# Six input weight columns: kept in DRAM for the second batch, or loaded and split again by it

## The chip, the core and the metric

The kernel runs on one core of one Trainium2 chip. The metric is the time of one execution on the device in microseconds. The engines are TensorE (PE; its weight loads are listed as PEld), VectorE (DVE), ScalarE (ACT), GpSimd (POOL) and SyncE (SP), which here only issues transfers. Each engine runs its own list of instructions in order and waits on semaphores for the others.

## What is computed

One layer of a hybrid encoder runs on two independent batches of 512 tokens, the prompt (b=0) and the sample (b=1), with the same weights. Cut to what matters here:

```python
mod = silu(c) @ w_ada + b_ada                     # (1, 6 * 1024)
sh1, sc1, g1, sh2, sc2, g2 = split(mod, 6)
h = rms_norm(x, norm1_g) * (1.0 + sc1) + sh1      # (512, 1024)
proj = h @ w_in                                   # w_in is (1024, 2816)
q_a, k_a, v_a, q_r, k_r, v_r, g_r = split(proj)   # 512, 128, 128, then 4 x 512 columns
o_a = windowed_attention(q_a, k_a, v_a, sink)
o_r = bidirectional_retention(q_r, k_r, v_r, g_r, decays)
x = x + g1 * (concat(o_a, o_r) @ w_out)
h = rms_norm(x, norm2_g) * (1.0 + sc2) + sh2
x = x + g2 * (square(relu(h @ w_mlp1)) @ w_mlp2)
y = rms_norm(x, final_g)
```

The first 768 columns of `w_in`, six blocks of 128, are the attention's: four of q, one of k, one of v. The change concerns these six blocks and nothing else.

## The kernel before, in words

**Products in three parts.** Every fp32 operand of a large product is split into two fp32r tensors, a high part (a cast of the value) and a low part (the value less the high part). A product is then three matmuls (`mm3`, lines 128 to 130): high by high, high by low, low by high. In the profile a weight block `k` therefore shows as `raw_k` (the load, line 89), `wh_k` (the cast on ScalarE, line 97) and `wl_k` (the subtraction on VectorE, line 103). The matmul at line 130 is the one that reads `wl`.

**The front.** For batch 0 the six attention blocks are computed first, in a front that goes through the 1024 rows of the weights in eight steps of 128 (`kc`). Each step loads one slab of 128 rows by 768 columns (`load_wi`), splits it into `wih` and `wil` (`split_wi`, lines 1029 to 1032), prepares one slab of `h` and adds 18 matmuls to six open PSUM banks (`products`, line 1046; in the profile the banks are named `first`). In between, the front makes the modulation vectors from `w_ada`: casts `wh_ada`, subtractions `wl_ada`, products `pm`, copies `mr` (line 221) and transposes `pmt` (line 229). The front's order is written out by hand and pinned for each engine (`pin`, line 76) up to its last steps.

**Keeping the splits.** When a step's products are issued, the front also stores the split slab of the step before (the last two at the end) into a DRAM tensor, `kept_first`. This is line 1055, two transfers of 384 KB for each of eight steps, issued from ScalarE's instruction list. The dictionary `kept` then maps the names of the six blocks to slices of that tensor.

**The rest of phase one.** After the front come the units of `run_units`: each loads its weights one unit ahead (`load`), then multiplies (`use`). For batch 0 these are the retention heads: value columns `rv`, and q, k, gate of heads 0 to 3 (`rq`, `rk`, `rg`). They load, split and also keep their blocks (`keep_unit`, line 112). Then batch 1 does its attention blocks, in the order k, v, q0 to q3 (`attn_units`, products `pj_k`, `pj_v`, `pj_q`), and its retention heads, all of which read the kept splits back (`kept_unit`, line 119: two loads of 512 KB each, the high part into the ring `ws` of four buffers, the low part into the ring `raw` of three).

Around the units a background of smaller work is woven in: batch 1's normalised input `h_1_0` to `h_1_7` (`px` transposes, `hm`, `h`), the retention scan of batch 0 (`prs` scores, `rsf` and `rsc` their decayed copies, `py` outputs, `ryt`, `pyn` transposes, `bn`, `mv`, `rva`, `rrs`, `ryn` their normalisation, `pyb`, `mix`), decay tables (`dtab`) and sums for the gate vectors on VectorE (`adacc_g`, with `raw_ada_g` from `w_ada`). Outside the pinned front a scheduler sets the order on each engine from the dependencies and from costs of its own, so an instruction that comes or goes there can move others.

Of the kernel before, what the change touches and what calls it, by code (L numbers as in the profile page):

```python
# [9 lines left out]
F32 = mybir.dt.float32  # L10
# [5 lines left out]
P = 128  # L16
# [3 lines left out]
KC = D // P  # L20
# [10 lines left out]
def trunk_kernel(ctx, tc, x0, x1, c0, c1, w_ada, b_ada, norm1_g, w_in, attn_sink, decay_f, decay_b,  # L31
                 w_out, norm2_g, w_mlp1, w_mlp2, final_g, y0, y1):
    nc = tc.nc
# [15 lines left out]
    def mm_bank(name):  # L49
        return psum.tile([P, 512], F32, tag="mm", name=name, bufs=3)  # L50
# [19 lines left out]
    def f(ap):  # L70
        return ap.bitcast(F32)
# [28 lines left out]
    def split_unit(src, name, lo_engine, pool=None):  # L100
        t = raw_unit(src, name)
        w = split_high(t, name, pool)
        lo_engine.tensor_sub(w[1], t, f(w[0]))  # L103
        return [x.rearrange("p (a n) -> p a n", n=src.shape[2]) for x in w]


    kept = {}

    def keep_unit(key, w):
        d = kept[key] = tc.dram_tile((P, 2, 1024), F32, name=f"kept_{key}")  # L110
        for s in range(2):
            nc.sync.dma_start(d[:, s, :], f(w[s]).rearrange("p a n -> p (a n)"))

    def kept_unit(key, name, n, lows=None):
        w = []
        for s in range(2):
            pool, tag, bufs = ((work, "ws", 4), lows or (work, "raw", 3))[s]
            t = pool.tile([P, 1024], F32R, tag=tag, name=f"w{'hl'[s]}_{name}", bufs=bufs)
            nc.sync.dma_start(f(t), kept[key][:, s, :])
            w.append(t.rearrange("p (a n) -> p a n", n=n))  # L120
        return w

    def cols_unit(wt, k0, nk, col, n):
        return wt[k0 * P:(k0 + nk) * P, col:col + n].rearrange("(k p) n -> p k n", p=P)

    def mm3(ps, lhs, rhs, start, stop):

        nc.tensor.matmul(ps, lhs[0], rhs[0], start=start, stop=False)  # L128
        nc.tensor.matmul(ps, lhs[0], rhs[1], start=False, stop=False)  # L129
        nc.tensor.matmul(ps, lhs[1], rhs[0], start=False, stop=stop)  # L130
# [20 lines left out]
    for r0, src in ((0, c0[0]), (8, c1[0]), (16, norm1_g[0]), (24, norm2_g[0]), (32, b_ada)):  # L151
        n = src.shape[0] // P
# [484 lines left out]
    def proj_unit(hT, col, name, done):  # L637
        key = f"in{col}"

        def load():  # L640
            if hT is hT_of[1]:
                return kept_unit(key, name, P)
            return split_unit(cols_unit(w_in, 0, KC, col, P), name, nc.vector)

        def use(w):
            bank = mm_bank(f"pj_{name}")
            for k in range(KC):
                mm3(bank, (w[0][:, k, :], w[1][:, k, :]), (hT[k][:, 0, :], hT[k][:, 1, :]), k == 0, k == KC - 1)
                if k == 3:
                    yield  # L650
            done(bank)
            yield
        return Unit(load, use, done, None if hT is hT_of[1] else lambda w: keep_unit(key, w))
# [32 lines left out]
    hT_of = [[], []]  # L686
# [295 lines left out]
    wi, pairs = {}, {}  # L982
# [64 lines left out]
    def products(kc, c0, c1):  # L1047
        w, h_ = wi[kc], hT[0][kc]
        for c in range(c0, c1):
            cs = slice(order[c] * P, (order[c] + 1) * P)  # L1050
            mm3(open_banks[c], (w[0][:, cs], w[1][:, cs]), (h_[:, 0, :], h_[:, 1, :]), kc == 0, kc == KC - 1)
        if c1 == 6:
            for k in ([] if kc == 0 else [kc - 1] if kc < KC - 1 else [kc - 1, kc]):
                for s in range(2):
                    nc.scalar.dma_start(kept_first[:, :, s, k * P:(k + 1) * P],
                                        f(wi[k][s]).rearrange("p (c n) -> p c n", n=P))

    kept_first = tc.dram_tile((P, 6, 2, 1024), F32, name="kept_first")
    for c in range(6):
        kept[f"in{c * P}"] = kept_first[:, c]  # L1060

    start = len(nc.cur_bb.bb.instructions)
    ones = []
# [6 lines left out]
    xT, hT = [], hT_of  # L1070
# [44 lines left out]
    open_banks = [(mm_bank if c < 3 else aux_bank)(f"first_{c}") for c in range(6)]  # L1115
    order = (4, 5, 0, 1, 2, 3)
    products(0, 0, 1)
    next(one1)
    products(0, 1, 2)
    next(one1)  # L1120
    for kc in range(6, KC):
# [3 lines left out]
    low_pair(2, 0, 0, nc.vector)  # L1125
    low_pair(2, 0, 1, nc.gpsimd)
    products(0, 2, 6)
    split_wi(2)
    load_pair(4)
# [363 lines left out]
```

## Time and profile before

| what | value |
|---|---|
| median of 3 runs | 1157.74 us (1156.06 to 1159.04) |
| the profiled execution's own time | 1156.6 us |
| its span on the core | 1154.8 us |
| TensorE busy, share of span | 1108.5 us, 96% |
| VectorE | 933.8 us, 81% |
| ScalarE | 494.8 us, 43% |
| moved by DMA | 231.71 MB, mean 201 GB/s |
| transfers issued by ScalarE (queue q10) | 6.29 MB in 12544 packets |

The profiled execution took 1.8 us more than its span, and 1.1 us less than the median of the runs. The front ends at about 83 us, batch 1's attention blocks are multiplied from about 222 us on, and its retention units end at about 403 us. Busy shares are means over these stages. A bracket behind a row of the timeline, as in `[0.70 <-issue]`, is the idle time of that engine ahead of the row and what ended it. Rows that start ahead of the end of the row above are pipelined.

### The profile page before, as it was taken

How to read it: one execution, taken by the hardware profiler on the slowest of the kernel's cores; microseconds unless marked ns; L12 is line 12 of the kernel's file. 1: busy time of each engine (PE TensorE's matmuls, PEld its weight loads, DVE VectorE, ACT ScalarE, POOL GpSimd, SP SyncE). 2: the span in 40 equal slices, each digit the busy share in tenths (PEclk: the TensorE clock that was granted, in tenths of full speed). 3: DMA queues.
4: the chain of work that ended last, by engine and by line, in shares of the span. 5: the costliest groups of instructions: out<-in, count | busy, mean ns of one | idle time of the engine just before them, and what ended most of it. 6: DMA issues, size and time to landing. Idle time of an engine off the chain costs nothing.

```text
span 1154.8 us, 14529 instructions
## 1 busy us (share of the span) xinstructions
PE 1108.5 (96%) x5167; PEld 903.3 (78%) x5167; DVE 933.8 (81%) x1557; ACT 494.8 (43%) x853; POOL 83.6 (7%) x107
## 2 busy tenths in 40 slices
PE   5989999999999999999999999999999999999985
PEld 3668787777888878888788888888778888888874
DVE  4888988988887697689988878879686875956996
ACT  4446765435563233345333423344454442431241
POOL 3620001100000000100000000023000000000012
PEclk9999999999999999999999999999999999999998
DMA  9786677665555589941655455446867264366713
GB/s 284 245 269 222 207 233 268 219 211 179 165 168 166 177 302 333 348 165 37 208 198 168 164 173 183 156 175 217 269 225 271 84 196 158 108 206 215 255 55 146
DMA packets 125344, 231.71 MB, mean 201 GB/s; under 512 B 8836, under 2 KB 60116, under 8 KB 125272
## 3 DMA queue, kind: packets, MB, share of 16 engines
q1 hardware_dynamic: 110136, 217.14, 55.9%
q0 software_dynamic: 2592, 7.37, 1.9%
q10 hardware_dynamic: 12544, 6.29, 1.9%
q8 instruction: 40, 0.66, 0.2%
q14 instruction: 32, 0.26, 0.1%
HBM read 156.03 MB, written 74.73 MB: 200 GB/s over the span
## 4 chain that ended last, share of the span: by engine, by line
PE 77%; DVE 11%; DMA 4%; issue 3%; ACT 2%; POOL 2%; DVEq 0%; POOLq 0%; ACTq 0%; SPq 0%
PE x L1324 14%; PE px_None L938 13%; PE py_None L938 10%; PE y L1324 9%; PE po L129 2%; PE po L130 2%; PE po L128 2%; PE po L429 2%; PE ppt L422 1%; PE psc L396 1%; PE pj_rq L130 1%; PE pj_rq L129 1%; PE pj_rq L128 1%; PE pj_rv L128 1%; PE pj_rv L130 1%
## 5 line engine op out<-in xcount | busy, mean ns | idle before, releaser
L128 PE MATMUL po<-wh_wo,ms 128*128 128x512 f32 x128 | 50.4, 397 | 1.5 <-ACT ms L761 1.5
L1324 PE MATMUL x<-wc_1h,uc_1h 128*128 128x512 f32 x128 | 50.0, 392 | 1.2 <-ACT wc_1h L843 1.2
L1324 PE MATMUL x<-wc_1l,uc_1h 128*128 128x512 f32 x128 | 50.1, 392 | 0.5 <-DVE wc_1l L844 0.5
L843 ACT CAST wc_0h<-w 128x1024 fp32r<-128x1024 f32 x24 | 25.2, 1049 | 59.2 <-PE x L1324 28.6
L129 PE MATMUL po<-wl_wo,ms 128*128 128x512 f32 x128 | 49.8, 391 | 0.6 <-DVE wl_wo L103 0.6
L1324 PE MATMUL x<-wc_1h,uc_1l 128*128 128x512 f32 x128 | 49.8, 389 | 0.0
L130 PE MATMUL po<-wh_wo,ms 128*128 128x512 f32 x128 | 49.6, 390 | 0.0
L255 DVE SCALAR_TENSOR_TENSOR adacc_c<-raw_ada_c,cact,adacc_c 128x512 f32<-128x512 f32 x56 | 39.8, 746 | 8.0 <-DMA raw_ada_c<-in_w_ada_dram 7.0
L843 ACT CAST uc_0h<-ur 128x1024 fp32r<-128x1024 f32 x21 | 22.1, 1051 | 52.6 <-PE x L1324 22.2
L406 ACT ACTIVATE st<-st,negm 128x256 f32<-128x256 f32 (+1 forms) x64 | 35.2, 555 | 18.5 <-DVE negm L401 18.5
L255 DVE SCALAR_TENSOR_TENSOR adacc_g<-raw_ada_g,cact,adacc_g 128x512 f32<-128x512 f32 x56 | 40.2, 745 | 2.1 <-DMA raw_ada_g<-in_w_ada_dram 1.7
L843 ACT CAST wc_s4h<-raw_w 128x1024 fp32r<-128x1024 f32 x16 | 16.8, 1052 | 56.9 <-PE px_None L938 32.4
L843 ACT CAST wc_1h<-w 128x1024 fp32r<-128x1024 f32 x24 | 25.1, 1047 | 36.1 <-DVE w L1302 21.0
L938 PE MATMUL py_None<-hch,wc_a 128*128 128x512 f32 x120 | 39.7, 390 | 0.1
L938 PE MATMUL px_None<-hch,wc_a 128*128 128x512 f32 x120 | 39.5, 390 | 0.0
L938 PE MATMUL px_None<-hch,wc_s 128*128 128x512 f32 x120 | 39.4, 389 | 0.0
L844 DVE TENSOR_TENSOR uc_0l<-ur,uc_0h 128x1024 fp32r<-128x1024 f32 x21 | 25.6, 1220 | 15.7 <-ACT uc_0h L843 15.7
L1324 PE MATMUL x<-wc_0h,uc_0h 128*128 128x512 f32 x96 | 37.5, 390 | 0.7 <-ACT u L959 0.7
L844 DVE TENSOR_TENSOR wc_0l<-w,wc_0h 128x1024 fp32r<-128x1024 f32 x24 | 29.3, 1220 | 10.9 <-ACT wc_0h L843 10.8
L1324 PE MATMUL x<-wc_0l,uc_0h 128*128 128x512 f32 x96 | 37.4, 389 | 0.0
L1324 PE MATMUL x<-wc_0h,uc_0l 128*128 128x512 f32 x96 | 37.4, 389 | 0.0
L1324 PE MATMUL y<-wc_1h,uc_1h 128*128 128x512 f32 x96 | 37.4, 389 | 0.0
(416 smaller groups left out, 3566.8 us busy)
## 6 DMA issues: line engine op xcount, KB each, us to landing
ur<-spill SPq DMA_DIRECT2D x49, 512.0 KB, 4.4
raw_w<-in_w_mlp_dram SPq DMA_DIRECT2D x32, 512.0 KB, 3.7
w<-in_w_mlp_dram SPq DMA_DIRECT2D x32, 512.0 KB, 6.8
spill<-s SPq DMA_DIRECT2D x56, 256.0 KB, 3.9
spill<-u SPq DMA_DIRECT2D x42, 256.0 KB, 2.5
raw_ada_g<-in_w_ada_dram SPq DMA_DIRECT2D x16, 512.0 KB, 4.6
raw_ada_c<-in_w_ada_dram SPq DMA_DIRECT2D x16, 512.0 KB, 4.2
raw_ada<-in_w_ada_dram SPq DMA_DIRECT2D x12, 512.0 KB, 8.8
```

Source lines behind the costliest of these rows:

```text
L128: nc.tensor.matmul(ps, lhs[0], rhs[0], start=start, stop=False)
L129: nc.tensor.matmul(ps, lhs[0], rhs[1], start=False, stop=False)
L130: nc.tensor.matmul(ps, lhs[1], rhs[0], start=False, stop=stop)
L255: nc.vector.scalar_tensor_tensor(acc[b], src, cb, acc[b], ALU.mult, ALU.add)
L396: nc.tensor.matmul(psc[:, :w], qs[hh][:, isl], k_[:, s, j0 * P:j1 * P], start=(s == 0), stop=(s == 1))
L406: nc.scalar.activation(st[hh][:, :w], st[hh][:, :w], AF.Exp, bias=negm[:, hh:hh + 1], scale=0.125, accum_out=den[:, hh:hh + 1])
L422: nc.tensor.transpose(pt[:, hh * P:(hh + 1) * P], st[hh][:, jj * P:(jj + 1) * P], ident)
L429: nc.tensor.matmul(po, va[:, j0 + jj, g].rearrange("p s e -> p (s e)"), pts[jj][:, s, :], start=(jj == 0 and s == 0), stop=(jj == nj - 1 a ...
L843: nc.scalar.copy(hi, src)
L844: nc.vector.tensor_sub(lo, src, f(hi))
L938: self.last = nc.tensor.matmul(bank[:, cs], x[:, k, :], y, start=first and k == 0 and i == 0, stop=last and k == 3 and i == 2, skip_group_ ...
L1324: nc.tensor.matmul(out, u[x][:, i % 2, ts_], w[y][:, i % 2, :], start=first and i == 0 and k == 0, stop=end and i == GP - 1 and k == 2, sk ...
```

## The change

The sixteen stores of line 1055 go, and with them the tensor `kept_first` and its six entries in `kept`. A block of batch 1 whose name is not in `kept` is now loaded from `w_in` and split like a block of batch 0; this holds for the six attention blocks. The retention blocks are still kept and read back.

```diff
         def load():
-            if hT is hT_of[1]:
+            if key in kept:
                 return kept_unit(key, name, P)
             return split_unit(cols_unit(w_in, 0, KC, col, P), name, nc.vector)
...
             mm3(open_banks[c], (w[0][:, cs], w[1][:, cs]), (h_[:, 0, :], h_[:, 1, :]), kc == 0, kc == KC - 1)
-        if c1 == 6:
-            for k in ([] if kc == 0 else [kc - 1] if kc < KC - 1 else [kc - 1, kc]):
-                for s in range(2):
-                    nc.scalar.dma_start(kept_first[:, :, s, k * P:(k + 1) * P],
-                                        f(wi[k][s]).rearrange("p (c n) -> p c n", n=P))
-
-    kept_first = tc.dram_tile((P, 6, 2, 1024), F32, name="kept_first")
-    for c in range(6):
-        kept[f"in{c * P}"] = kept_first[:, c]
```

Both parts of a split block now lie in the ring `ws` of four buffers, so two blocks are in flight, and the raw block lies in `raw`. Six loads of 512 KB from `w_in` stand in place of twelve from `kept_first`; ScalarE gets six casts, VectorE six subtractions. TensorE has the same products.

The scheduler moves much between 83 us and some 310 us. Three places are shown. The first is TensorE from the transposes `pyn_1` of batch 0's retention on to the first products of batch 1. Before, from the last two `pj_rg` rows on, the scores `prs` and `pj_k`:

```order
L129 MATMUL pj_rg_3_2306<-h_0_7_742,wh_rg_3_2223 128x512
L130 MATMUL pj_rg_3_2306<-h_0_7_742,wl_rg_3_2224 128x512
L128 MATMUL prs_2_1_2361<-rq_2_1925,rk_2_1996 128x512
L129 MATMUL prs_2_1_2361<-rq_2_1925,rk_2_1996 128x512
L130 MATMUL prs_2_1_2361<-rq_2_1925,rk_2_1996 128x512
L128 MATMUL pj_k_2384<-h_1_0_1967,wh_k_2376 128x512
L129 MATMUL pj_k_2384<-h_1_0_1967,wh_k_2376 128x512
L130 MATMUL pj_k_2384<-h_1_0_1967,wl_k_2378 128x512
L128 MATMUL pj_k_2384<-h_1_1_2004,wh_k_2376 128x512
L129 MATMUL pj_k_2384<-h_1_1_2004,wh_k_2376 128x512
L130 MATMUL pj_k_2384<-h_1_1_2004,wl_k_2378 128x512
```

After, from `pyn_1` on:

```order
L476 MATMUL pyn_1_2302<-ident,ryt_1_2267 128x128 x4
L128 MATMUL pj_rg_3_2289<-h_0_7_733,wh_rg_3_2206 128x512
L129 MATMUL pj_rg_3_2289<-h_0_7_733,wh_rg_3_2206 128x512
L130 MATMUL pj_rg_3_2289<-h_0_7_733,wl_rg_3_2207 128x512
L128 MATMUL prs_2_1_2344<-rq_2_1908,rk_2_1979 128x512
L129 MATMUL prs_2_1_2344<-rq_2_1908,rk_2_1979 128x512
L130 MATMUL prs_2_1_2344<-rq_2_1908,rk_2_1979 128x512
L128 MATMUL pj_k_2371<-h_1_0_1950,wh_k_2361 128x512
L129 MATMUL pj_k_2371<-h_1_0_1950,wh_k_2361 128x512
L128 MATMUL pj_v_2453<-h_1_0_1950,wh_v_2367 128x512
L130 MATMUL pj_k_2371<-h_1_0_1950,wl_k_2362 128x512
L128 MATMUL pj_k_2371<-h_1_1_1987,wh_k_2361 128x512
```

Before, twelve `pj_rg` rows, of which the last two are shown, and three `prs` rows stood between `pyn_1` and `pj_k`; now three `pj_rg` rows do, and a first row of `pj_v` stands ahead of the first that reads `wl_k`.

The second place is VectorE in the same stretch, where `rva_1` ends the statistics of `pyn_1`. Before:

```order
L455 TENSOR_TENSOR rsc_2_0_2300<-rsf_2_0_2298,rsc_2_0_2300 128x512
L481 BN_AGGR mv_1_2324<-bn_1_3_2334 128x2
L255 SCALAR_TENSOR_TENSOR adacc_g_1_1_2214<-raw_ada_g_1_1_2370,cact,adacc_g_1_1_2214 128x512
L483 TENSOR_SCALAR rva_1_2337<-mv_1_2324 128x4
L560 TENSOR_SCALAR dtab_3_2438<-dl,lg 128x896
L488 TENSOR_SCALAR ryn_1_2341<-pyn_1_2319,mv_1_2324,rrs_1_2339 128x128 x4
L380 SCALAR_TENSOR_TENSOR rg_3_2358<-rg_3_2358,pj_rg_3_2306 128x512
L452 SCALAR_TENSOR_TENSOR rsf_2_1_2365<-prs_2_1_2361,dtab_2_2287 128x512
```

After:

```order
L455 TENSOR_TENSOR rsc_2_0_2283<-rsf_2_0_2281,rsc_2_0_2283 128x512
L481 BN_AGGR mv_1_2307<-bn_1_3_2317 128x2
L255 SCALAR_TENSOR_TENSOR adacc_g_1_1_2197<-raw_ada_g_1_1_2353,cact,adacc_g_1_1_2197 128x512
L483 TENSOR_SCALAR rva_1_2320<-mv_1_2307 128x4
L103 TENSOR_TENSOR wl_k_2362<-raw_k_2359,wh_k_2361 128x1024
L488 TENSOR_SCALAR ryn_1_2324<-pyn_1_2302,mv_1_2307,rrs_1_2322 128x128 x4
L380 SCALAR_TENSOR_TENSOR rg_3_2341<-rg_3_2341,pj_rg_3_2289 128x512
L452 SCALAR_TENSOR_TENSOR rsf_2_1_2348<-prs_2_1_2344,dtab_2_2270 128x512
L103 TENSOR_TENSOR wl_v_2368<-raw_v_2365,wh_v_2367 128x1024
```

`wl_k` stands behind `rva_1` in place of `dtab_3`, which comes six rows later, and `wl_v` behind `rsf_2_1`. The rows from the first `bn` of `pyn_1` to `rva_1`, of which these show the last, are the same in both orders.

The third place is ScalarE a little earlier, around the last `h` blocks of batch 1. Before:

```order
L327 CAST h_1_5_2185<-hm_1_5_2186 128x512
L291 COPY adacc_g_0_1_1056<-pg_0_1_2208 1x512
L253 ACTIVATE adacc_g_1_0_2213<-raw_ada_g_1_0_2215,cact 128x512
L253 ACTIVATE adacc_g_1_1_2214<-raw_ada_g_1_0_2215,cact 128x512
L454 CAST rsc_1_3_2205<-rsf_1_3_2203 128x512
L327 CAST h_1_6_2248<-hm_1_6_2249 128x512
L333 CAST rk_3_2268<-pj_rk_3_2230 128x512
L472 COPY ryt_1_2284<-py_1_1903 128x512
```

After:

```order
L291 COPY adacc_g_0_1_1039<-pg_0_1_2191 1x512
L327 CAST h_1_5_2168<-hm_1_5_2169 128x512
L97 CAST wh_k_2361<-raw_k_2359 128x1024
L253 ACTIVATE adacc_g_1_0_2196<-raw_ada_g_1_0_2198,cact 128x512
L253 ACTIVATE adacc_g_1_1_2197<-raw_ada_g_1_0_2198,cact 128x512
L454 CAST rsc_1_3_2188<-rsf_1_3_2186 128x512
L327 CAST h_1_6_2231<-hm_1_6_2232 128x512
L333 CAST rk_3_2251<-pj_rk_3_2213 128x512
L472 COPY ryt_1_2267<-py_1_1886 128x512
```

`wh_k` now stands between `h_1_5` and the first rows of the `adacc_g_1` sums, ahead of `rsc_1_3`, `h_1_6`, `rk_3` and `ryt_1`. It needs the buffers that head 3's `rk` block leaves.

## Prediction

> **What bounds the kernel now.** I began with the profile page: the busy share of each engine, the DMA queue that the change empties, and the chain that ended last.
>
> ```profile
> PE 1108.5 (96%) x5167; PEld 903.3 (78%) x5167; DVE 933.8 (81%) x1557; ACT 494.8 (43%) x853; POOL 83.6 (7%) x107
> ...
> q10 hardware_dynamic: 12544, 6.29, 1.9%
> ...
> PE 77%; DVE 11%; DMA 4%; issue 3%; ACT 2%; POOL 2%; DVEq 0%; POOLq 0%; ACTq 0%; SPq 0%
> ```
>
> TensorE is busy 96% of the span and holds 77% of the chain, so a microsecond of work on another engine counts only where TensorE comes to wait for it. The 6.29 MB of q10 are what the front stores (8 rows x 2 x 384 KB); their packets took 1.9% of the span. Next I read the busy time by stages (columns: stretch, length, PE, PEld, DVE, ACT, POOL, PE clock, DMA share, GB/s).
>
> ```profile
> 42.00:68.00 26.00, 22.63 (x125) 16.19 (x124) 20.76 (x31) 11.16 (x18) 12.76 (x6) 1.00 0.78 236
> 180.00:210.00 30.00, 28.76 (x142) 22.20 (x141) 27.24 (x52) 15.86 (x28) 4.02 (x5) 1.00 0.72 244
> 210.00:240.00 30.00, 30.00 (x141) 24.48 (x141) 28.33 (x53) 12.92 (x21) 1.90 (x2) 1.00 0.54 180
> ```
>
> The change touches two places. In the front (42 to 68 us) TensorE idles 26.00 - 22.63 = 3.4 us in all. Around the start of batch 1's attention (210 to 240 us) it doesn't idle, while VectorE works 27.24 + 28.33 = 55.57 of 60 us. Third, what TensorE waited for in the front (42 to 83 us, two rows), and then from 83 to 330 us:
>
> ```profile
> PE pmt L229 <- ACT mr L221: 2.4, 2, 2.1
> PE first L129 <- DVE h L328: 0.9, 1, 0.9
> ```
>
> ```profile
> PE pj_rk L130 <- DVE wl_rk L103: 0.8, 1, 0.8
> PE pj_rv L128 <- DVE mix L494: 0.7, 1, 0.7
> PE px L312 <- DVE rv_x L304: 0.5, 1, 0.5
> ```
>
> No attention product of batch 1 waits for a weight today. The three longest waits behind the front sum to 2.0 us.
>
> **Removed: the sixteen stores of the front.** They are issued by ScalarE:
>
> ```profile
> L1055 ACTq DMA_DIRECT2D kept_first<-wih x8: 520/521/1124, 46.3 to 77.7; - x8
> L1055 ACTq DMA_DIRECT2D kept_first<-wil x8: 520/786/1875, 47.0 to 78.3; - x8
> ```
>
> By the medians these are 8 x 0.52 + 8 x 0.79 = 10.5 us of issue. Most of it lies where ScalarE had nothing to do: in its timeline only these rows were held by an issue:
>
> ```profile
> 47.60 1.05 ACT L97 CAST wh_ada<-raw_ada 128x1024 fp32r<-128x1024 f32 x1 [0.70 <-issue]
> 63.95 1.04 ACT L97 CAST wh_ada<-raw_ada 128x1024 fp32r<-128x1024 f32 x1 [0.23 <-issue]
> 79.82 0.53 ACT L514 ACTIVATE bias_t<-di 128x384 bf16<-128x384 f32 x1 [1.03 <-issue]
> ```
>
> The first sits ahead of an `mr` that TensorE waited 0.3 us for (2.4 us in two waits, less the longer of 2.1), and the second ahead of the 2.1 us one. So 0.3 us there, about 0.2 at the second, and up to 0.2 from the `wl_ada` that follows the first cast: **-0.7 us**. The third has no waiting TensorE behind it. Bounds: 0, if other operands are just behind, and -3.4 us, all the idle time of that stretch. The moved bytes need no term of their own: neither wait above names a DMA, and the six loads of 512 KB that replace twelve only halve what batch 1 loads.
>
> **Added: six splits, and an order that makes TensorE meet them.** The nearest operations are the retention weights' splits, of the same shape (min/median/max ns):
>
> ```profile
> L97 ACT CAST wh_rq<-raw_rq x4: 1035/1046/1057, 108.0 to 186.2; 128x1024 fp32r<-128x1024 f32 x4
> L103 DVE TENSOR_TENSOR wl_rq<-raw_rq,wh_rq x4: 1214/1218/1220, 112.2 to 193.6; 128x1024 fp32r<-128x1024 f32 x4
> ```
>
> That is 6 x 1.05 = 6.3 us on ScalarE, which is 43% busy, and 6 x 1.22 = 7.3 us on VectorE, four of them (4.9 us) in the stretch where it had 60 - 55.57 = 4.4 us free. What they cost is read from the place where the first is needed. Before, on TensorE:
>
> ```profile
> 213.16 0.39 PE L130 MATMUL pj_rk<-h,wl_rk 128*128 128x512 f32 x1
> ...
> 217.95 0.60 PE L476 MATMUL pyn<-ident,ryt 128*128 128x128 f32 x4
> 218.30 0.48 PE L128 MATMUL pj_rg<-h,wh_rg 128*128 128x512 f32 x1
> ...
> 220.47 0.39 PE L128 MATMUL pj_rg<-h,wh_rg 128*128 128x512 f32 x1
> ...
> 222.29 0.39 PE L130 MATMUL pj_k<-h,wl_k 128*128 128x512 f32 x1
> ```
>
> One matmul follows another every 0.23 us, and `pj_k`'s first use of `wl_k` comes without a wait. VectorE at that time:
>
> ```profile
> 218.74 0.29 DVE L480 BATCH_NORM_STATS2 bn<-pyn 128x6 f32<-128x128 f32 x1
> ...
> 222.98 0.17 DVE L483 TENSOR_SCALAR rva<-mv 128x4 f32<-128x4 f32 x1
> 223.05 0.68 DVE L560 TENSOR_SCALAR dtab<-dl,lg 128x896 f32<-128x896 f32 x1
> 224.66 1.36 DVE L488 TENSOR_SCALAR ryn<-pyn,mv,rrs 128x128 f32<-128x128 f32 x4 [0.93 <-POOL rrs L485]
> ```
>
> In the new order `wl_k` stands directly behind `rva`, in place of that `dtab`, and everything from the first `bn` to `rva` stands ahead of it as before, 223.05 - 218.74 = 4.31 us without a gap. So `wl_k` is ready 4.31 + 1.22 = 5.53 us after that `bn`, which itself can only follow `pyn`. On TensorE nine matmuls now stand between `pyn` and the first use of `wl_k`: three `pj_rg`, three `prs`, two `pj_k`, one `pj_v`. Nine matmuls behind `pyn` bring the old row to 220.47, that is 220.47 - 217.95 = 2.5 us from `pyn`'s start. VectorE's `bn` began 218.74 - 217.95 = 0.8 us after `pyn`'s start, some 0.4 us of it needed for the first of the four transposes. TensorE's wait is then 0.4 + 5.53 - 2.5 = 3.4 us at the least, 0.8 + 5.53 - 2.5 = 3.8 us if VectorE is as late as before.
>
> It will be later, through the new ScalarE order: `wh_k` stands ahead of the two `adacc` starts, of `rsc` and `h`, and must wait until the last `pj_rk` has left its buffer (of the four of that ring). Before, they ran as follows:
>
> ```profile
> 209.65 1.33 ACT L253 ACTIVATE adacc_g<-raw_ada_g,cact 128x512 f32<-128x512 f32 x2
> 211.43 0.62 ACT L454 CAST rsc<-rsf 128x512 fp32r<-128x512 f32 x1 [0.45 <-DVE rsf L452]
> ```
>
> Counted from the last `pj_rk`'s end (213.16 + 0.39 = 213.55), `rsc` started 2.1 us ahead of it; now it starts 1.05 + 1.33 = 2.4 us behind it. Queued behind `wh_k` on ScalarE are also `h`, `rk` and `ryt`, and on VectorE all that needs these, up to `bn`. TensorE reaches `pyn` later too: 29 matmuls and four transposes from that `pj_rk` (29 x 0.23 + 0.35 = 7.0 us), where it was 217.95 - 213.39 = 4.6. Walking VectorE's rows from there with the durations of before, `bn` comes about 2.0 us after `pyn` could feed it: 3.4 + 2.0 = 5.4 us. I take **+5.0 us** (3.4 to 5.7), nearer the upper end, because VectorE's stretch has almost no free time, and part of the lateness may be caught up.
>
> **A second wait.** The next product that needs VectorE soon is `py`, which needs the `rsc` ending VectorE's backlog. Before:
>
> ```profile
> 238.92 1.29 DVE L455 TENSOR_TENSOR rsc<-rsf,rsc 128x512 fp32r<-128x512 f32 x2
> ...
> 243.70 1.42 DVE L255 SCALAR_TENSOR_TENSOR adacc_g<-raw_ada_g,cact,adacc_g 128x512 f32<-128x512 f32 x2 [0.77 <-DMA raw_ada_g<-in_w_ada_dram]
> ```
>
> ```profile
> 241.14 0.39 PE L130 MATMUL py<-rsc,rv 128*128 128x512 f32 x1
> ```
>
> From `ryn` to the end of `rsc` was 240.2 - 224.66 = 15.5 us. The new order puts in that stretch three splits (3 x 1.14, as a following row starts some 0.08 us before the end), the displaced `dtab` (0.6) and four `adacc` that came later (2 x 1.42 = 2.8, or 2.7 back to back), less 0.4 us of old idle: some 21.5 us. TensorE from the first use of `wl_k` to that `py` took 241.14 - 222.29 = 18.9 us, and now has about seven matmuls more in between (1.6 us), 20.4. Difference: **+1.2 us** (0 to 2.5). The last two splits, `wl_q_2` and `wl_q_3`, stand among `bn` and `adacc` rows where VectorE is freer (240 us on): **+0.5** (0 to 1).
>
> **The clock.** A pause can cost more than itself. Here TensorE lost its clock once behind a short one:
>
> ```profile
> 36.96 0.28 PE L216 MATMUL pm<-wl_ada,c 128*4 128x256 f32 x1 [1.77 <-DVE wl_ada L1009]
> ```
>
> ```profile
> 38.00:40.00 2.00, 2.00 (x10) 1.36 (x9) 2.00 (x2) 0.21 (x1) 2.00 (x2) 0.50 0.00 0
> 40.00:42.00 2.00, 2.00 (x8) 1.22 (x7) 1.93 (x4) 0.58 (x2) 1.66 (x1) 0.71 0.74 208
> ```
>
> It ran at 0.50 for 2 us and 0.71 for 2, a loss of 1.0 + 0.6 = 1.6 us; yet the 2.1 us wait in 42 to 68 us left the clock at 1.00. A 5 us pause lies beyond both, so 0 to 1.6 us; I take **+0.8**, the middle, as the two rows contradict each other.
>
> [...]
>
> **The sum.** Some of the 2.0 us of old waits behind the front will be swallowed by the new pause or reordered away: -0.4 (0 to -2.0). -0.7 + 5.0 + 1.2 + 0.5 + 0.8 - 0.4 = **+6.4 us**. On the profiled execution (1156.6 us, of which the span is 1154.8) that is 1163.0; the median of the runs is 1157.74, 1.1 us above it, so 1164.1. A measurement here can tell about 0.3% from no change, 3.5 us.
>
> **The rivals.**
> *No change that can be told.* VectorE catches up before `bn`, TensorE finds `wl_k` earlier than the order suggests, and only the smaller waits stay: 1157.74 - 0.7 + 1.2 + 0.5 = 1158.7, up to 1161.2. For it: two of ScalarE's held rows end with the stores, and the lateness behind `wh_k` is walked, not shown. Against: the 3.4 us hold even with VectorE idle at `bn`. Chance 0.25.
> *Faster.* The mechanism is the front: the stores' bytes and issues hold more than the profile attributes to them, with the DMA engines 78% busy in 42 to 68 us, and the whole 3.4 us of idle time there falls away, besides 2.0 us of waits behind it: 1157.74 - 5.4 = 1152.3. It decides only if `wl_k` is also on time, since 3.4 us there eats the front's bound. Against: no wait in the front names a DMA. Chance 0.12.
> *Slower than forecast.* VectorE never regains the 7.3 us before the retention of batch 1 starts, so all of it ends on TensorE, with the clock's 1.6 and two thirds of a microsecond at the last splits: 1157.74 + 7.3 + 1.6 + 0.7 - 0.7 = 1166.6, with both upper bounds of the waits 1169. Chance 0.18, inside "slower".
> *The forecast itself*, one long wait before `pj_k` and a short one at `py`: 0.45.
>
> That the splits aren't made is no case: the order holds six more casts and six more subtractions.
>
> **The numbers.** Slower 0.45 + 0.18 = 0.63, same 0.25, faster 0.12. The range runs from 1156.0 (the no-change case with a front worth some 2 us more; what lies below is about 0.12) to 1169.0.
>
> **What would show it.** Right: TensorE waits for `wl_k` of 3.4 to 5.7 us at the first `pj_k` L130, released by VectorE, followed by a row at a clock below 1.00; a wait at `py` for `rsc`; the front's `mr` waits shorter by 0.5 us in sum; ScalarE's `wh_k` late after `pj_rk`. Wrong: no wait at `pj_k`, or a `bn` that starts within 0.5 us of `pyn` so that the wait is 3.4 at most; front waits that shrink by over 2 us; or waits of batch 1 that name a load of `raw_k`, whose landing I held to be early.

## The result, and the profile after

The changed kernel takes 1164.9 us (median of six runs, 1163.59 to 1165.85), beside 1157.45 us before (six runs, 1156.06 to 1159.04): a ratio of 1.0059, interval 1.0047 to 1.0072, or 7.5 us more. The forecast was 1164.1 us. The profiled execution took 1165.34 us, its span 1163.5 us, which is 8.7 us over the span before. Medians and ratios are taken over the executions in the chip's usual state; of all runs in this document, only two of the twelve executions with the sums left out (1862 and 2254 us) fall outside it.

From the page of the changed kernel, the busy shares and the chain that ended last:

```profile
PE 1112.8 (96%) x5167; PEld 905.8 (78%) x5167; DVE 941.4 (81%) x1563; ACT 500.2 (43%) x859; POOL 85.4 (7%) x107
...
PE 74%; DVE 14%; DMA 4%; issue 4%; ACT 3%; POOL 2%; SPq 0%; DVEq 0%; POOLq 0%; ACTq 0%
```

VectorE and ScalarE have six instructions more each, and 7.6 and 5.4 us more busy time. TensorE has the same 5167 matmuls, and its share of the chain falls from 77% to 74% while VectorE's rises from 11% to 14%. The busy time by stages (columns as in the prediction):

```profile
42.00:68.00 26.00, 23.04 (x129) 16.30 (x128) 21.38 (x32) 12.01 (x19) 13.79 (x6) 1.00 0.43 131
180.00:210.00 30.00, 29.45 (x141) 22.75 (x140) 26.25 (x51) 16.43 (x27) 4.63 (x6) 1.00 0.80 278
210.00:240.00 30.00, 25.20 (x110) 19.76 (x111) 29.02 (x52) 13.58 (x21) 2.43 (x2) 0.89 0.36 110
```

The front gains 0.4 us of TensorE's idle time, and the DMA engines are 43% busy there in place of 78%. The stretch from 210 to 240 us, which had no idle time on TensorE, now has 4.8 us of it, and the clock is at 0.89. The waits of TensorE, from 42 to 83 us, and then from 83 to 330 us:

```profile
PE pmt L229 <- ACT mr L221: 1.8, 1, 1.8
PE first L128 <- ACT h L327: 1.7, 2, 0.9
PE first L129 <- DVE h L328: 1.3, 3, 0.8
```

```profile
PE pj_v L128 <- ACT wh_v L97: 3.5, 1, 3.5
PE pj_k L130 <- DVE wl_k L103: 1.3, 1, 1.3
PE py L128 <- ACT rsc L454: 0.5, 1, 0.5
```

The `mr` waits shrink from 2.4 to 1.8 us, but new waits for `h` come up. Behind the front a wait of 3.5 us at `pj_v` and one of 1.3 us at `pj_k` stand side by side. In the changed kernel's timeline, all engines:

```profile
220.57 0.60 PE L476 MATMUL pyn<-ident,ryt 128*128 128x128 f32 x4
...
223.05 0.29 DVE L480 BATCH_NORM_STATS2 bn<-pyn 128x6 f32<-128x128 f32 x1
...
224.88 0.62 ACT L454 CAST rsc<-rsf 128x512 fp32r<-128x512 f32 x1 [0.78 <-DVE rsf L452]
...
225.41 1.04 ACT L97 CAST wh_v<-raw_v 128x1024 fp32r<-128x1024 f32 x1
...
226.50 0.79 PE L128 MATMUL pj_v<-h,wh_v 128*128 128x512 f32 x1 [3.47 <-ACT wh_v L97]
...
227.29 0.16 DVE L483 TENSOR_SCALAR rva<-mv 128x4 f32<-128x4 f32 x1
227.36 1.21 DVE L103 TENSOR_TENSOR wl_k<-raw_k,wh_k 128x1024 fp32r<-128x1024 f32 x1
...
228.62 0.80 PE L130 MATMUL pj_k<-h,wl_k 128*128 128x512 f32 x1 [1.33 <-DVE wl_k L103]
```

VectorE's `bn` starts 2.5 us behind `pyn`, and `wl_k` 4.31 us behind `bn` (227.36 - 223.05), without a gap. `wh_v` stands on ScalarE behind `rsc`, which waits for VectorE's `rsf`: so both waits, 3.47 + 1.33 = 4.80 us, come from the same late VectorE, and had `wh_v` been early, `wl_k` alone would still have held TensorE until 228.6. How much the whole stretch costs is read at the end of the retention, from the last matmul of its kind, before and after:

```profile
L130 PE MATMUL pj_rg<-h,wl_rg x24: 387/389/476, 347.8 to 402.7; 128*128 128x512 f32 x24
```

```profile
L130 PE MATMUL pj_rg<-h,wl_rg x24: 387/389/476, 355.1 to 410.0; 128*128 128x512 f32 x24
```

It starts 7.3 us later: nearly the whole difference of the medians lies ahead of 410 us.

### The profile page after: what moved, and what is told of

The parts are those of the page before. It is cut to its first block, busy times and chain, and to the rows that moved or that the text cites. A ratio compares the mean times of both kernels' runs of the same rounds, so it can differ in the third digit from the quotient of the medians.

```text
span 1163.5 us, 14514 instructions
## 1 busy us (share of the span) xinstructions
PE 1112.8 (96%) x5167; PEld 905.8 (78%) x5167; DVE 941.4 (81%) x1563; ACT 500.2 (43%) x859; POOL 85.4 (7%) x107
## 4 chain that ended last, share of the span: by engine, by line
PE 74%; DVE 14%; DMA 4%; issue 4%; ACT 3%; POOL 2%; SPq 0%; DVEq 0%; POOLq 0%; ACTq 0%
PE x L1315 14%; PE px_None L938 13%; PE py_None L938 9%; PE y L1315 9%; PE po L129 2%; PE po L130 2%; PE po L128 2%; PE psc L396 1%; PE ppt L422 1%; PE po L429 1%; PE pj_rv L128 1%; PE pj_rv L130 1%; PE pj_rv L129 1%; DMA x<-in_x_prompt_dram 1%; PE pj_rq L128 1%
## 5 line engine op out<-in xcount | busy, mean ns | idle before, releaser
L1315 PE MATMUL y<-wc_1h,uc_1l 128*128 128x512 f32 x96 | 37.4, 389 | 0.0
```

The source lines that it names most:

```text
L1315: nc.tensor.matmul(out, u[x][:, i % 2, ts_], w[y][:, i % 2, :], start=first and i == 0 and k == 0, stop=end and i == GP - 1 and k == 2, sk ...
```

## Experiments

Two theories stood against each other at first. **By order**: TensorE meets `wl_k` too early, because the order puts it behind VectorE's normalisation; another place for it, or another engine, gives most of the loss back. **By room**: VectorE has no free time for the splits around 210 to 280 us, and its lateness comes out somewhere, whatever the order. A third point was what the stores themselves cost. The first edit is shown against the kernel before, the others against the changed kernel; `...` marks lines left out. Ratios are to the kernel before on the same chip; these medians of before were 1156.6 us for the first four, 1155.64 for the next four, 1155.45 for the three behind those and 1155.43 for the last.

### Stores kept, splits added

```diff
-            if hT is hT_of[1]:
+            if key in kept:
...
-    for c in range(6):
-        kept[f"in{c * P}"] = kept_first[:, c]
```

> Here the front stores as before (nobody reads the stores) and batch 1 splits its six blocks itself. In its order wl_k again stands directly behind rva on VectorE, but twelve pj_rg rows instead of three stand between pyn and pj_k on TensorE, and wh_k stands later on ScalarE, behind rsc and h. My theory (TensorE waits for a split that the order puts behind a long VectorE row of work, so the wait is 4.31 + 1.22 us less the matmuls in between): the nine more matmuls (2.1 us) and the earlier bn take the wait from 4.8 us to 1.0 to 2.5 us, too short for the clock to fall, and the time is 1158.5 to 1161.5. Rival A (the six splits are work that must be paid wherever they stand, and the order only chooses the place): the time is that of the changed kernel, 1163.5 to 1166. Rival B (the loss comes from the front, whose weight splits moved up when the stores went and held TensorE 2.4 us): with the stores back it is gone, 1157 to 1159, with or without a wait at pj_k.

1160.2 us, ratio 1.0027 (1.0012 to 1.0042), as the theory by order had expected. The clock stayed at 1.00 from 222 to 232 us, the stretch of the wait; that a wait of up to 2.5 us is too short for it to fall, no run shows: before, it fell behind one of 1.77 us (last section). TensorE waits for `wl_k` once (from 83 to 330 us, the two longest):

```profile
PE pj_k L130 <- DVE wl_k L103: 1.6, 1, 1.6
PE ppt L422 <- ACT st L414: 1.5, 1, 1.5
```

The same six splits cost about half of what they cost in the changed kernel, so the stores' removal, or the order that comes with it, makes the other half.

### Neither stores nor splits

```diff
-            if key in kept:
-                return kept_unit(key, name, P)
+            if hT is hT_of[1]:
+                return kept_unit("rv0", name, P)
```

Every block of batch 1's attention is read from one kept value block, so this kernel leaves out the right weights and is for timing alone.

> No stores in the front and no splits in batch 1: its six blocks read twelve halves of 512 KB from another kept block, so the attention of batch 1 is computed with wrong weights; the instructions and their shapes are those of before without the stores. It has the front of the changed kernel, with the value weights' splits moved up. My theory: no wait at pj_k, the front is up to 2.4 us late at 85 to 120 us and catches this up at the old waits of 125 and 182 us, so 1156.0 to 1158.5, no difference from before that could be told. Rival B (the front): 1159 to 1161. A rival C (the stores cost more than the profile showed): under 1155.

1155.59 us, ratio 0.9994 (0.9983 to 1.0004). Without the stores, and with twelve loads of 512 KB from a kept block in the place of the splits, as many as before, nothing is gained that can be told. By the interval, the stores and what they moved in the order cost at most 0.2%.

### All low parts of these units on GpSimd

```diff
-            return split_unit(cols_unit(w_in, 0, KC, col, P), name, nc.vector)
+            return split_unit(cols_unit(w_in, 0, KC, col, P), name, nc.gpsimd)
```

> The changed kernel with the low parts of the six blocks subtracted on GpSimd, which is busy 7% of the span, at some 2.5 us each by the wl_ada rows of the front. wl_k then waits only for wh_k, so no wait at pj_k. But wl_v stands ahead of the normalisation's rrs on GpSimd, and waits for wh_v, which stands behind rsc on ScalarE: I expect TensorE to wait 1 to 2.5 us at pyb, whose ryn waits for rrs. My theory: 1157.5 to 1160.5. Rival A (the work has to be paid): 1163 or more, as GpSimd is slower and slows VectorE beside it.

1171.26 us, ratio 1.0131 (1.0113 to 1.0149), where 1157.5 to 1160.5 was expected: a miss. The edit reached further than meant, since the retention's q, k and gate blocks of batch 0 take the same line, twelve splits more. So the ratio doesn't speak for the six alone. But it showed one reason why GpSimd is little relief, in this kernel's timeline, and for the same operation of VectorE in the timeline of before:

```profile
119.07 2.40 POOL L103 TENSOR_TENSOR wl_rk<-raw_rk,wh_rk 128x1024 fp32r<-128x1024 f32 x1 [7.76 <-ACT wh_rk L97]
...
119.54 1.95 DVE L401 TENSOR_SCALAR negm<-mx 128x4 f32<-128x4 f32 x1
```

```profile
93.50 0.17 DVE L401 TENSOR_SCALAR negm<-mx 128x4 f32<-128x4 f32 x1
```

The row of four elements ends only when GpSimd's subtraction does (119.54 + 1.95 = 121.49; 119.07 + 2.40 = 121.47).

### q kept, k and v split

The stores and the entries in `kept` come back for the four q blocks alone.

```diff
+                    nc.scalar.dma_start(kept_first[:, 0:4, s, k * P:(k + 1) * P],
+                                        f(wi[k][s])[:, 0 * P:4 * P].rearrange("p (c n) -> p c n", n=P))
...
+    for c in range(0, 4):
+        kept[f"in{c * P}"] = kept_first[:, c]
```

> The four q blocks are kept as before (stores of 4/6 of the size), k and v are split by batch 1. The order around pj_k is that of the kernel with both stores and splits. My theory: the wait at pj_k of 1.0 to 2.5 us is there in full, the later one at py is not; 1158 to 1160.5, within 1 us of the kernel with all six splits and stores. Rival A (cost per split): a third of the changed kernel's loss, about 1160, but spread, and at least 2 us less than in the kernel with six splits and stores.

1163.4 us, ratio 1.0061 (1.0045 to 1.0078). The waits in this kernel, from 195 to 330 us and from 42 to 90 us:

```profile
PE pj_k L130 <- DVE wl_k L103: 1.6, 1, 1.6
```

```profile
PE first L128 <- ACT h L327: 2.8, 2, 1.9
```

The wait at `pj_k` came as expected, but the time did not (1158 to 1160.5 expected): here the front's new waits for `h` (the second of them, 1.93 us, followed by a halved clock; granted over the whole span 0.992, before 0.994) were not regained. With four blocks fewer to split nothing was given back; but the run mixes two causes and decides nothing by itself.

### Only the low part of k on GpSimd

```diff
-            return split_unit(cols_unit(w_in, 0, KC, col, P), name, nc.vector)
+            return split_unit(cols_unit(w_in, 0, KC, col, P), name, nc.gpsimd if hT is hT_of[1] and col == 512 else nc.vector)
```

> The changed kernel with one subtraction moved: wl_k of batch 1 alone is made on GpSimd, some 2.4 us by its rows in the earlier run. All orders up to pj_k are those of the changed kernel, with nine fewer matmuls than before between pyn and pj_k and wh_k at its place; pj_k's 24 rows now stand together, ahead of the first pj_v. wh_k ended at 214.4 us and TensorE came to wl_k at 222.9, so wl_k is ready long before. My theory (the loss is the wait for wl_k and wh_v behind VectorE's long row, and the clock after it): no wait over 0.5 us at pj_k, no slow clock there, and of the 4.8 + 2 us at least 4 come back, 1157.5 to 1161; what is left is at pyb or py, up to 2 us, since GpSimd's subtraction stretches VectorE's rows beside it. Rival A (the splits have to be paid wherever they are): over 1163.

1165.23 us, ratio 1.0083 (1.0067 to 1.0098): against the theory by order, which had expected 1157.5 to 1161. The wait left `pj_k` and came up at `pj_q`; 0.4 us stayed at `pj_v`:

```profile
PE pj_q L130 <- DVE wl_q L103: 4.5, 1, 4.5
...
PE pyb L493 <- DVE ryn L488: 0.9, 2, 0.6
```

### The order of the front as before

The stores' absence let the scheduler put the splits of the first value blocks (`wh_rv`, `wl_rv`) ahead of the last slabs of `h`. Here they are tied behind the front's last instruction on their engine, which `front_last` holds.

```diff
+                if kq < 2:
+                    for i in list(nc.cur_bb.bb.instructions)[n0:]:
...
+                            tc.add_manual_dep(i, front_last[i.engine].name, mybir.DependencyInfo(
+                                mybir.DependencyClass.NoSync, mybir.DependencyReason.DATA), reason="order")
```

> The changed kernel, in which the casts and subtractions of the first two value blocks are tied behind the front's last instruction on ScalarE and VectorE, as they stood before the change. The order at pj_k stays that of the changed kernel (four pj_rg rows behind pyn instead of three). My theory: the front's waits for h at 74 and 80 us go (2.2 us), but that lag had been caught up at the old waits of 125 and 182 us by the time of pj_k, so the end is the same within 1 us, 1163.5 to 1166, with the same wait of 4 to 5 us at pj_v and pj_k. Rival B (the front's order is the loss, or a part of it): 1161 to 1162.7.

1162.28 us, ratio 1.0059 (1.0045 to 1.0074). The front's waits for `h` fell from 3.0 to 0.8 us (one for `ks` behind it rose from 0.3 to 1.2), the waits of 3.2 us at `pj_v` and 1.3 us at `pj_k` stayed, and the ratio is that of the first comparison. The time itself lies in the range that had been given to the front (1161 to 1162.7), but the kernel before was 1.8 us faster on this chip too, so the ratio decides. The front's order is not the main cause; since the changed kernel gave 1.0059 on one chip and 1.0078 on another (below), a share of up to 0.2% isn't excluded.

### k and v kept, q split

As in the run with q kept, with `kept_first[:, 4:6]` and the blocks 4 and 5.

> k and v are kept by the front (stores of a third of the size), the four q blocks are split by batch 1. Like the kernel that kept q, its front has the value blocks' casts ahead of the last h, so TensorE waits about 3 us there; whether that is caught up depends on the order behind it (caught up in the changed kernel, not in the one that kept q). My theory: no wait at pj_k; waits of under 1.5 us in sum at py and later; so 1157 to 1158.5 if the front's lag is caught up and 1159.5 to 1161 if not. Rival A (four of six splits, two thirds of the loss, about 5 us): 1161 or more without a lag from the front.

1162.57 us, ratio 1.0058 (1.0043 to 1.0074), over the 1161 that had been expected at most. `pj_k` and `pj_v` had nothing to wait for, and the wait came later:

```profile
PE pj_q L130 <- DVE wl_q L103: 3.3, 1, 3.3
```

In the front, an `mr` wait of 2.69 us, with a halved clock behind it (granted over the whole span 0.990, before 0.994), is part of this time.

### Own buffers for k and v

```diff
+            early = hT is hT_of[1] and col in (512, 640)
+            return split_unit(cols_unit(w_in, 0, KC, col, P), name, nc.vector, spare_ws if early else None)
```

> The changed kernel with the split k and v in buffers of their own, so that wh_k and wh_v need not wait for the buffers of the retention's last units. The order then puts wh_k and wh_v behind the scan's rsc on ScalarE, wl_k and wl_v still later on VectorE, and on TensorE the transposes pyb_1 and ten more matmuls ahead of pj_k. If the ring of four buffers were the cause, the wait would be gone: 1157 to 1159. My theory: the cause is VectorE's row between the first bn and ryn with too few matmuls beside it, so the wait moves to pyb, which needs ryn: TensorE reaches it some 1.8 us after pyn's start and ryn is ready some 6.5 us after it, 4 to 5 us of wait and the clock behind it, 1162.5 to 1166.

1165.82 us, ratio 1.0088 (1.0073 to 1.0103). `wh_k` no longer depends on `pj_rk` leaving its buffer, but the scheduler now puts it later on ScalarE (230.74 us in place of 213.30) and `wl_k` later on VectorE (231.95 in place of 227.36), and TensorE waits at another place, longer:

```profile
PE pyb L493 <- DVE ryn L488: 7.1, 2, 6.9
```

So the wait stood at `pj_v` and `pj_k` in the changed kernel, at `pj_q` in two others and at `pyb` here, and none of the four ratios is below 1.0058. In these four the order chose where TensorE meets VectorE's lateness, not whether. This run by itself doesn't decide between the theories: the one by order had forecast the wait at `pyb` too (4 to 5 us), and it ends at 228.08 us, ahead of the first of the six subtractions.

### The gate sums behind the splits, alone and with the front's order

If the order alone is at fault, twelve `adacc_g` rows that compete with the splits on VectorE could stand behind them, where they are not yet needed.

```diff
...
+    for kq, low in {1: 'k1', 2: 'q1_0', 3: 'q1_1'}.items():
+        for i in sums[kq]:
+            tc.add_manual_dep(i, lows[low].name, mybir.DependencyInfo(
+                mybir.DependencyClass.NoSync, mybir.DependencyReason.DATA), reason="order")
```

> The changed kernel with the same work, in which twelve VectorE rows of the gate sums (adacc_g_1, 0.67 us each, whose result is needed some 50 us later) are tied behind splits: the second four behind wl_k, the third behind wl_q_0, the last behind wl_q_1. Where the split of k, its product and the splits of q stood behind up to six of these rows, wl_k now stands ahead of the first bn, and five rows separate it from what it needs. My theory, as it stands after the earlier runs (the splits cost nothing where VectorE's rows ahead of them can wait; the loss is the order, in which rows that could wait stand ahead of rows that TensorE waits for): no wait over 1 us at pj_k, pj_v or pj_q, no slow clock there, up to 1.5 us in sum at pyb and py, and 1156.5 to 1159.5 by the scale of the kernel before at 1156.5 (ratio 1.000 to 1.003). Rival A (VectorE has no room from 195 to 245 us, so the four splits there, 4.6 us, must come out as waits whatever the order): a wait of 3 to 5 us at another product, such as pj_q, and a ratio of 1.005 or more.

> The kernel with the gate sums behind the splits, and besides the first two value blocks' splits tied behind the front, as in the run with the front's order restored. My theory: the front's waits for h (2.2 us) go, but their lag was mostly caught up behind it, so 0 to 1 us better than the kernel with the sums alone: ratio 0.999 to 1.002 to the kernel before. Rival B (the front's lag is a loss of its own): 2 us better than with the sums alone.

> The changed kernel as it is, on the chip of the two above, to set them beside it: ratio 1.005 to 1.007, with 4 to 5 us of waits at the first pj_v and pj_k.

Here `sums` holds those rows and `lows` each split's subtraction. The sums alone: 1162.94 us, 1.0060 (1.0047 to 1.0072). With the front's order as well: 1160.9 us, 1.0047 (1.0035 to 1.0059). The changed kernel on the same chip: 1163.99 us, 1.0078 (1.0066 to 1.0090). The theory had expected 1.000 to 1.003 of the first and 0.999 to 1.002 of the second, and missed both; of the third 1.005 to 1.007. With the sums alone the long wait is gone and no clock was lost at that place (1.00 from 222 to 232 us), but TensorE still waited, in small pieces (from 215 to 300 us):

```profile
PE pyb L497 <- DVE ryn L492: 2.0, 2, 1.1
PE pj_rv L128 <- DVE qs L378: 0.8, 1, 0.8
PE pyn L480 <- ACT ryt L476: 0.7, 1, 0.7
```

With five more they sum to 5.6 us, 0.7 us of it for a load. What the tie gave back, 0.0018 of the ratio or 1.05 us between the medians, has intervals that overlap, and neither it nor the front's part, 0.0013 between the first two, can be told from nothing.

### Twelve gate sums left out

The theory by room was now: with less work on VectorE in that stretch, in the order that the scheduler gives without it, the loss goes. The kernel leaves twelve terms of one gate vector out, and is for timing alone.

```diff
-                    else:
+                    elif name != "g2_1" or kq == 0:
```

> The kernel with the gate sums behind the splits, but with those twelve VectorE rows left out (their loads stay), so that half of one gate vector is summed over a quarter of its terms only and the output is not the reference's. TensorE's and VectorE's orders around pj_k are otherwise those of that run: wl_k ahead of the first bn, three pj_rg rows behind pyn. VectorE has 12 x 0.67 = 8.0 us less to do between 220 and 265 us. Theory as it stands now: VectorE is some 5 us late already at ryn of head 0 (208 where it was 203 us), has no room for the splits until 275 us, and its lateness comes out as waits whatever the order. With 8.0 us of its work gone, more than the six splits' 7.3, the small waits at pyb, pyn, pvt and pj_rv, 5.4 us in sum, fall below 2 us, VectorE's ryn of head 3 is back near 270 us (278 with the sums), and the ratio to the kernel before is 0.999 to 1.002. Rival D (the rest of the loss is in ScalarE's casts, in the loads of raw weights or in the scan's own chain): VectorE idles for the 8 us, TensorE's waits stay at 4 us or more, and the ratio at 1.004 or more.

1155.98 us (median of ten executions), ratio 1.0007 (0.9995 to 1.0019): as expected. The six splits are all made, no store is made, and 8.0 us of sums are missing on VectorE. TensorE's two largest waits from 195 to 330 us are now

```profile
PE ppt L422 <- ACT st L414: 1.0, 1, 1.0
PE pyb L493 <- DVE ryn L488: 0.5, 2, 0.2
```

Up to `wl_k` VectorE's order is here that of the run with the sums tied, where `wl_k` stands ahead of the first `bn` too, and that run, with the sums in, took 1.0060. So it is not this place of `wl_k` that gives the loss back: with 8.0 us less work VectorE has the room that the splits lack. Two things stay open: further on the two orders differ, and the sums were not left out of the kernel before, where TensorE's waits from 195 to 330 us, 1.2 us in all, bound what that could gain there. No kernel tried here beat the one before by more than can be told.

## Why the prediction came out right, and where its reasons failed

**The bound moves to VectorE for one stretch.** The landmarks are VectorE's first and last `ryn` of batch 0's retention. Before, from 203.19 to 268.86 us; after, from 208.46 to 278.88. The busy time between them, of before and of after, and then with the sums left out (207.03 to 270.02):

```profile
203.19:268.86 65.67, 65.32 (x305) 52.16 (x304) 55.72 (x110) 26.88 (x45) 4.97 (x6) 1.00 0.61 205
```

```profile
208.46:278.88 70.42, 65.10 (x295) 51.54 (x294) 64.10 (x121) 32.14 (x51) 5.51 (x6) 0.95 0.45 140
```

```profile
207.03:270.02 62.99, 62.78 (x295) 50.42 (x294) 56.39 (x109) 32.23 (x51) 5.02 (x6) 1.00 0.51 161
```

Before, TensorE fills its stretch (65.32 of 65.67 us). After, it has ten matmuls fewer to do between the landmarks, and idles 5.3 us. VectorE is busy 64.10 of 70.42 us. Of the 6.3 us left, the brackets of its rows name 5.6: 2.6 us for GpSimd's `rrs`, which itself needs VectorE's `rva`, 2.8 us for ScalarE, 0.2 us for TensorE. With 7.7 us less on VectorE the same 295 matmuls fit in 7.4 us less, and TensorE is full again (62.78 of 62.99).

**Why the splits cost less with the stores kept.** VectorE's work from 83 to 195 us, before and after:

```profile
83.00:195.00 112.00, 110.12 (x544) 89.89 (x543) 100.66 (x230) 79.01 (x174) 3.90 (x5) 1.00 0.70 233
```

```profile
83.00:195.00 112.00, 111.08 (x546) 90.29 (x545) 96.32 (x224) 76.51 (x170) 3.04 (x4) 1.00 0.65 212
```

In the order without stores VectorE has done 4.3 us less by 195 us, six instructions, though TensorE is no slower in this window. Counted from the span's start the debt is smaller, 3.6 us (159.72 against 156.14), as some of the work was done ahead of 83 us. Without splits it costs nothing, since VectorE makes up for it (the run with neither: 60.5 us between the same two `ryn`). With splits it can't, and the debt falls due together with them. The run with stores and splits has next to no debt in that window (100.25 us). Its first `ryn` starts at 203.65 us, 0.5 later than before, where the changed kernel is 5.3 late; from there to the last `ryn` it takes 70.76 us, about as long as the changed kernel. That the debt and the splits add up is argued from these rows; no run took the debt away alone.

**Point by point.**

- *The wait for `wl_k`, +5.0 us: measured 4.80, in two pieces, and 5.5 us in all.* `bn` came 2.5 us behind `pyn`'s start where 2.0 + 0.4 were walked, and from `bn` to `wl_k` it was 4.31 us to the hundredth. I overlooked that `wh_v` stands on ScalarE behind a `rsc` that waits for VectorE, so TensorE met ScalarE's name first. The sum stays, since `wl_k` ends 8.0 us behind `pyn`'s start, as forecast (0.4 + 2.0 + 5.53). From the row ahead of the pause (222.64) to the first use of `wl_k` (228.62) it is 5.98 us, where two rows take 0.46: besides the two waits, 0.7 us goes into the lone `pj_v` row (0.79 us, at a clock of 0.50) and the row before it, which nothing overlaps.
- *The reason given for it fell.* The prediction made it a matter of place: `wl_k` behind `rva`. Moving it, its engine, its buffers or its neighbours moved the wait, and the ratios of these kernels lie between 1.0047 and 1.0088. The condition that decides was in the prediction as a side remark, 4.9 us of splits for 4.4 us of free time on VectorE, and as the mechanism of the rival "VectorE never regains the 7.3 us", whose own time, 1166.6, came out 1.7 us too long.
- *The second wait at `py`, +1.2: measured 0.5; the last splits, +0.5: no wait that names them.* TensorE, held up once, came later to all that follows, so most of the second wait was paid already. The terms given for it (15.5 + 3 x 1.14 + 0.6 + 2.7 - 0.4) make 21.8 us and not 21.5, so its own rows forecast 1.4.
- *The clock, +0.8: measured 1.7.* The eight intervals of `pj_k` rows behind the pause took 3.55 us where 1.84 is usual. The prediction took the middle between a full loss and none; behind all eight waits of 2.69 us or more up to 410 us the rows ran at half speed (last section), so of its range the 1.6 us end was near the measured loss.
- *The front, -0.7: it was there, and was turned round.* TensorE was 0.8 us ahead at 69 us, 0.3 of it an earlier start. Then the scheduler's new order, which the prediction had not looked at there, cost more, as the timeline behind the front's modulation shows:

```profile
69.17 1.22 DVE L103 TENSOR_TENSOR wl_rv<-raw_rv,wh_rv 128x1024 fp32r<-128x1024 f32 x1
...
73.34 0.62 ACT L327 CAST h<-hm 128x512 fp32r<-128x512 f32 x1 [3.81 <-DVE hm L326]
...
74.01 0.50 PE L128 MATMUL first<-h,wih 128*128 128x512 f32 x1 [0.77 <-ACT h L327]
```

  `wl_rv` stands ahead of `h` on VectorE, and TensorE waits for `h`; its first `pj_rv` starts 1.6 us later than before (84.53 against 82.90), a swing of 2.4 us. Up to the first `pj_k` most of the lag is regained, since the old waits at 125 and 182 us (1.8 us in all) had slack in them: it starts 0.6 us later than before (222.40 against 221.84), with the same 997 matmuls behind it. So the front, forecast at -0.7, came out at +0.6, with those old waits already used up. The run with neither stores nor splits has waits for `h` in the front too (2.1 us) and a ratio of 0.9994.
- *The sum.* +0.6 at the first `pj_k`, 5.5 for the pause, 1.7 for the clock and 0.5 at `py`, less 0.7 of old waits behind it that are gone, make 7.6 us, beside 7.3 measured at the end of the retention. Later, 1.9 us more at 862 us, 0.3 of it a longer wait and 1.6 the clock (last section), bring the profiled difference to 8.7, while the medians differ by 7.5. The forecast of +6.4 met this because its errors cancel: the front and the old waits together (-1.1 forecast, -0.1 measured) were 1.0 us too low, the pause 0.5 and the clock 0.9, while `py` was 0.7 and the last splits 0.5 too high. That the median came out within 0.8 us is in part luck; the place and the size of the long wait are not.
- *The rivals.* "Faster through the front" is out by the run with neither; "no change" needed a VectorE that catches up, and it doesn't.

Stores issued by SyncE were not tried.

## What to carry to other kernels

When a change moves work to an engine off the critical path, compare its busy time with its free time over the stretch in which the work must be done, and use two landmarks of that engine, not one wait: a wait that changes its place with every reordering and doesn't go away (4.8, 4.5 and 7.1 us with all six splits here) points to a backlog, and leaving out work there, for timing alone, is the test. Without new free time, the orders tried here could move the wait or spread it, and none removed it. And look at what the scheduler does with the hole that the removed instructions leave, also where nothing was added.

## What the runs showed of the hardware

**Waits of about 2 us were followed by a halved clock in some executions and not in others; counted on a grid of 3.41 us, the two kinds part.** In the changed kernel at 862 us two waits close together, 1.51 and 0.53 us, were followed by it; before, the waits at the same place were of 1.20 and 0.53 us, and the rows behind them took 0.39 us as usual. The changed kernel:

```profile
861.59 0.73 PE L1315 MATMUL x<-wc_1h,uc_1h 128*128 128x512 f32 x2 [1.51 <-ACT wc_1h L843]
862.85 0.50 PE L1315 MATMUL x<-wc_1l,uc_1h 128*128 128x512 f32 x1 [0.53 <-DVE wc_1l L844]
...
864.11 0.63 PE L1315 MATMUL x<-wc_1h,uc_1l 128*128 128x512 f32 x1
```

From 863.68 us on rows take 0.63 us in place of 0.39. Of seventeen waits between 1.79 and 2.13 us in the profiles of this case (from 20 us on), eight were followed by rows at half speed and nine were not. Longer waits don't settle it either: all eight of 2.69 us or more up to 410 us were, but of the wait of 3.03 or 3.04 us that every profile has near its end, nine were and five were not.

In the profiles of before and after the slow stretches are 3.41 us long, or twice that (225.29 to 232.12 us in the changed kernel), but for the one that runs to the end of each. Within a profile they start a whole number of 3.413 us apart: in the changed kernel at 37.56, 225.29, 863.58 and 1133.24 us, which is 55, 187 and 79 such windows. Counted on this grid, the two rows that the prediction couldn't reconcile differ. Before, the window of the 1.77 us wait at 36.96 us and the next one, and then the two windows over which the wait of 2.09 us at 66.26 us is split (columns as in the prediction):

```profile
34.33:37.74 3.41, 1.64 (x12) 0.86 (x11) 3.34 (x5) 2.09 (x3) 1.72 (x2) 1.00 0.22 81
37.74:41.15 3.41, 3.41 (x15) 1.99 (x13) 3.41 (x2) 0.79 (x2) 3.41 (x2) 0.50 0.20 35
```

```profile
61.64:65.05 3.41, 2.53 (x17) 1.69 (x14) 1.95 (x5) 2.15 (x4) 0.72 (x1) 1.00 0.79 181
65.05:68.46 3.41, 2.20 (x14) 1.44 (x14) 3.41 (x2) 1.58 (x3) 2.44 (x1) 1.00 1.12 356
```

The first leaves TensorE busy for 1.64 of 3.41 us, and the clock is at 0.50 in the next; the others leave it busy for 2.53 and 2.20, and it stays at 1.00. In the fourteen profiles, from 20 us on, all 39 windows at full clock with more than 1.79 us of idle time were followed by a slow one, none with less than 1.66 us was, and of the 24 in between eleven were. In the profiles of before and after, the eight that a slow one followed left TensorE idle for 1.76 us or more, about half of 3.41 us, and none of the others for more than 1.51. From this an estimate: a pause of 4.8 us puts at least 2.4 us into one window wherever the grid lies, and one of 2 us comes to 1.76 only when nearly all of it falls into one window. The two losses of the changed kernel, 1.7 us at 226 us and 1.6 at 862, are half of some 3.5 us of slow rows each. Its runs differ by about as much (1163.59 to 1165.85 us); that such losses make this difference is an estimate too.

**Beside a subtraction on GpSimd some of VectorE's rows took longer, and others did not.** The `negm` row, 0.17 us in the kernel before, took 1.95 us beside GpSimd's `wl_rk`, and that subtraction itself took 2.40 us where VectorE takes 1.22. The front of before has both kinds beside GpSimd's `wl_ada` (49.68 to 52.16 us): a copy `m` took 0.17 us at 50.24, and the row behind it, `ms`, took 1.75 us and ended at 52.19, where the `ms` at 41.79 us, with no GpSimd row beside it, took 0.16. What parts the two kinds is not shown.
